# One chunk of the ffn ring and four of the mixer ring moved onto the split weights' 128 byte lines, and products of ones placed at six waits of TensorE

## The chip, the cores and the metric

The kernel runs on one core of a Trainium2 chip, in one launch. The metric is device microseconds of that launch, the median of several runs; lower is better. The notes below call the engines as the profile does: PE is TensorE (matmuls), PEld its weight loads, DVE VectorE, ACT ScalarE, SP the engine that issues most of the DMAs.

## What is computed

A sequence of 256 tokens with 1024 channels goes through two models one after the other, in fp32. Cut to what matters here:

```python
# first_block: a gmlp layer, then an attention layer, each followed by a mixture of experts
x = x + g1 * gmlp_mixer(modulate(rmsnorm(x), sh1, sc1), ...)       # layer 0
x = x + g2 * moe(modulate(rmsnorm(x), sh2, sc2), ...)              # 64 experts, 8 per token
x = x + g1 * moba_mixer(...)                                       # layer 1: attention over 256 keys
x = x + g2 * moe(...)
x = rmsnorm(x) * final_norm
# second_block, twice:
x = x + 0.5 * swiglu_ffn(rmsnorm(x), w_up, w_down)                 # 1024 -> 2 x 2816 -> 1024
x = x + hybrid_mixer(rmsnorm(x), ...)                              # pooling + gated linear recurrence
x = x + 0.5 * swiglu_ffn(rmsnorm(x), w_up, w_down)
# and a last rmsnorm
```

## The kernel before

**Order of the work.** The program is one list of items, emitted in order: gmlp, the experts of layer 0 (moe), attention, the experts of layer 1, then for each of two layers an ffn, the hybrid mixer and a second ffn. Each item names the weights that it reads, its PE work and what follows on ACT and DVE. PE executes its instructions in the order of this list and waits at each for its operands, so whatever is emitted ahead of a waiting matmul runs ahead of it. Channels lie on the 128 partitions, the 256 tokens on the free axis.

**Weights.** They stream from HBM through SP's queue into a ring of nine slots of 1 MB (line 177). For the dense layers each slot is split into a rounded high part `WH` (an ACT copy, line 243) and a low part `WL` (a DVE subtraction, line 246), two halves of 1024 columns each. A product is then three matmuls of 128 x 128 weights by 128 x 256 moving data: `WH` by the activations' high part, `WH` by their low part, `WL` by their high part (`mm3`, line 290; all go through `mm`, line 288).

**Where operands lie.** `ring`, `WH`, `WL` and `x` are whole multiples of 128 bytes per partition. After them comes a pad of 64 bytes (`pad0`), then `hH` and `hL`, the split input of a stage (8 chunks of 256 tokens each, 1 KB per chunk), then a second pad of 64 bytes. `hH` and `hL` therefore lie half of a 128 byte line off from `WH` and `WL`. The arena `rarena`, allocated last, also lies half a line off (the offsets that the change adds rest on that). Its views begin at multiples of 1 KB or of 128 bytes, so all of them are half a line off too. Among them are the ring of an ffn's hidden chunks, `hid_ring(0, 6)` (line 543): six chunks of high parts, then six of low parts; the mixer's rings `vH, vL` (ten chunks, also used for `yH, yL`) and `pH, pL` (four chunks, also used for `mH, mL`); and `SHU1`, in which the moe keeps half of the shared expert's up weights, as weights this time (line 729).

**An ffn** (`swiglu_items`, line 785) has 22 up items of 48 matmuls, which read `hH, hL`, and 11 down items of 48 matmuls (`down_d`, line 396), which read chunks 2i and 2i+1 (mod 6) of the ring: for every down but the last, first the 24 matmuls of the even chunk, then the 24 of the odd one. Chunk 0 is so read by downs 0, 3, 6 and 9. Downs and ups alternate, one down to two ups.

**The mixer** (`hybrid`, line 1584): projections from `hH, hL`; `smallA`, which reads v chunks 0 to 5 (six matmuls each); `smallB`, which reads v chunks 6 to 9 and the four p chunks; the pool-up items, which read p; then `lru_up`, where each of eight output chunks is a sum over the ten y chunks in order (30 matmuls), and the out projection, which reads the m chunks.

**Moe.** For each block of tokens the gather (line 1097) multiplies by `WH`-side weights with moving data in `rarena`. The shared expert's `shared_mm` (line 1039) uses, for j = 2 and 3, weights from `SHU1` with `hH, hL` as moving data: the one place where weights and moving data are both half a line off.

**Waits of PE around the change.** In gmlp, PE waits between the first vector-matrix products and the first projection, while DVE and ACT make `hH, hL` (`mod_h`, line 367). In each routing stage it waits for DVE to choose the experts (line 938) ahead of `route1b` (line 940). At the end of layer 1's moe (`scat_last`, line 1184) it waits for the first chunk of the first ffn's input. At the start of attention it waits three times: ahead of the sums of squares (`stat_mm`), ahead of the row of inverse roots (`stat_row`), and ahead of the first chunk that `norm` makes (line 1319).

Of the kernel before, what the change touches and what calls it, by code (L numbers as in the profile page):

```python
# [18 lines left out]
T = 256  # L19
# [1 line left out]
KD = 8  # L21
NRING = 9
FW = 6656
RW = 7168
HCAP, MCAP, LCAP = 10, 9, 9
RMS_EPS = 1e-6
LN_EPS = 1e-5
# [67 lines left out]
def moba_moe_hybrid_kernel(ctx: ExitStack, tc: tile.TileContext, A: dict):  # L95
# [50 lines left out]
    def rview(off, n):  # L146

        assert off + n <= RW, (off, n)
        return rarena[:, off:off + n]
# [42 lines left out]
    def add(pe, post=(), slots=(), lead=0, fence=(), nsplit=2):  # L192
        post = [] if post is None else [post] if callable(post) else list(post)
        items.append(Item(list(slots), pe, post, st["nring"], fence, lead, nsplit))
# [95 lines left out]
    def mm3(out, w, h, l, start, stop, swap=False):  # L290
        wh, wl = w
        for j, (a, b) in enumerate(((wh, h), (wh, l), (wl, h))):
            if swap:
                a, b = b, a
            mm(out, a, b, start and j == 0, stop and j == 2)

    def to_hl(src, H, L):
        S.copy(H, src)  # L298
        V.tensor_sub(L, src, H)  # L299
# [36 lines left out]
    def stat_mm(sqs, b=STB):  # L336

        for m in range(KD):
            c = 32 * (m % 4)
            mm(PB[b][c:c + 32, :T], ones[:, :32], sqs[m], m < 4, m >= 4, tile_position=(0, c))  # L340
# [12 lines left out]
    def stat_row(p=None):  # L353
        p = PB[STB][:, :T] if p is None else p
        for t in range(2):
            P.transpose(p[:, t * 128:(t + 1) * 128], nv[:, 1, t:t + 1].to_broadcast([128, 128]), ident)
        S.copy(R, p)
# [9 lines left out]
    def mod_h(Ac, Bc, H, L, ks=range(KD)):  # L367

        ts = {}

        def low(k):
            V.scalar_tensor_tensor(L[:, k], ts.pop(k), Bc[:, k:k + 1], H[:, k], op0=ALU.add, op1=ALU.subtract)
        for i, k in enumerate(ks):
            t = ts[k] = tmp512()[:, :T]
            V.scalar_tensor_tensor(t, x[:, k], Ac[:, k:k + 1], R, op0=ALU.mult, op1=ALU.mult)
            S.activation(H[:, k], t, AF.Identity, bias=Bc[:, k:k + 1])
            if i:
                low(ks[i - 1])
        low(ks[-1])
# [147 lines left out]
    def add_all(lst):  # L527
        for it in lst:
            add(*it)
# [13 lines left out]
    def hid_ring(off, n):  # L543
        Hs = rview(off, n * T).rearrange("p (n t) -> p n t", n=n)
        Ls = rview(off + n * T, n * T).rearrange("p (n t) -> p n t", n=n)
        return Hs, Ls

    def gmlp():
        v = spare(5, 4096).rearrange("p (t f) -> p t f", t=2)
        u = spare(5, 4096, 4096).rearrange("p (m t) -> p m t", m=16)  # L550
# [30 lines left out]
        for i, it in enumerate(first):  # L581
            add(*(it + (None, ()))[:3], nsplit=0)
            if i == 1:
                add(stats, nsplit=0)
                add(lru_consts, nsplit=0)
        add(load, nsplit=0)

        add(lambda: scale_cols(0, sc1(0), "nmix", 0), nsplit=1)
        add(lambda: mod_h(Acol[:, 0], sh1(0), hH, hL))
# [259 lines left out]
    def moe(l, tail):  # L849
# [162 lines left out]
        side = gemv_items(3, adac[:, 1, 0:16], "adab", 48, 5) if l == 0 else gemv_half(1, g2(1), "adab", 88, 5)  # L1012
        g0, g1_ = ((4, 4), (0, 0))[l]
        add_all(side[:g0])
        add(route1b)
        add_all(side[g0:g1_])
        add(route2)
# [166 lines left out]
        def scat_last(tail):  # L1184
            def pe():
                b = NB - 1
                for k in range(KD):
                    fs = slice(k * 128, (k + 1) * 128)
                    for j, y in enumerate((yH, yL)):
                        mm(PB[4 + k // 2][:, k % 2 * T:(k % 2 + 1) * T], y[:, fs], STm[:, b % 3], j == 0, j == 1)  # L1190
                tail(lambda k: upd(k, PB[4 + k // 2][:, k % 2 * T:(k % 2 + 1) * T]))
            add(pe, fence={yb // 2}, nsplit=l)

        def scat(b):
# [51 lines left out]
        def upd(k, y):  # L1246
            V.scalar_tensor_tensor(x[:, k], y, g2(l)[:, k:k + 1], x[:, k], op0=ALU.mult, op1=ALU.add)
# [53 lines left out]
    def attention():  # L1301
# [16 lines left out]

        def norm():
            stat_row()  # L1320
            mod_h(Acol[:, 1], kvc[:, 0:8], kvH, kvL)

        side = gemv_items(4, adac[:, 1, 16:32], "adab", 64, 0) + gemv_half(0, sc2(1), "adab", 80)
# [3 lines left out]
        def gemvs(m, nsplit=2):  # L1327
            nonlocal n
            for it in side[n:n + m]:
                add(*(it + (None, ()))[:3], nsplit=nsplit)  # L1330
            n += m

        gemvs(3, 0)
        add(lambda: stat_mm(sqs_of["x"]), nsplit=0)
        add(stat_sum, nsplit=0)
        add(norm)
        ring_slots(0, 1, 2, 3, 4)

# [214 lines left out]
            V.scalar_tensor_tensor(x[:, k], x[:, k], cols[:, o + k:o + k + 1], R1, op0=ALU.mult, op1=ALU.mult)  # L1553

    def first_ffn(fin):
        hidH, hidL = hid_ring(0, 6)
        sums = lambda: (stat_mm(sqs_of["x"]), stat_mm(sqs_of["y"], 1))
        lst = swiglu_items("f1u", 0, "f1d", 0, 22, hidH, hidL, evac_R, fin, 6,
                           [{"korder": True, "before": lambda: sqs_of["first"]()}, {"after": sums}, {"mid": first_sums}, {"mid": first_rows, "bank": 3}], lag=4)
        for i, n in enumerate((8, 10, 12, 14)):  # L1560
            pe, post, slots, lead = lst[n]
            lst[n] = (pe, list(post or []) + [lambda i=i: first_x(2 * i, 2 * i + 1)], slots, lead)
        add_all(lst)
# [13 lines left out]
            nc.sync.dma_start(A["out"][k], y)  # L1577

    def ffn(l, which, fin):
        hidH, hidL = hid_ring(0, 6)  # L1580
        nm = f"f{which}"
        add_all(swiglu_items(nm + "u", 22 * l, nm + "d", 11 * l, 22, hidH, hidL, evac_R, fin, 6))

    def hybrid(l, fin):
# [5 lines left out]
        gates = spare(6, 4096).rearrange("p (n f) -> p n f", n=8)  # L1590
        up_ = spare(6, 2 * 288, 5376).rearrange("p (b t) -> p b t", b=2)
        pw = spare(6, 4 * 288, 4096).rearrange("p (b t) -> p b t", b=4)
        vH, vL = hid_ring(0, 10)
        yH, yL = vH, vL
        pH, pL = hid_ring(5120, 4)
        mH, mL = pH, pL
        sp4 = lruc[:, 5, l * 10:(l + 1) * 10]
        nsp8 = lruc[:, 0, l * 10:(l + 1) * 10]
# [310 lines left out]
```

## Time and profile before

| | |
|---|---|
| three timed runs | 2549.05, 2557.68, 2557.32 us; median 2557.32 |
| the profiled execution's own time | 2549.97 us |
| its span, first to last instruction | 2548.0 us |
| PE busy | 2421.7 us (95%) |
| DVE, ACT busy | 1359.7 us (53%), 1041.7 us (41%) |
| HBM read | 720.50 MB |
| mean granted TensorE clock | 0.988 of full speed |

Times in the profile are microseconds from the start of the span. A view of windows gives, for each stretch, the busy time of each engine with the number of instructions, then the clock that was granted to TensorE (1.00 is 2.4 GHz, 0.50 is 1.2 GHz), the share of the DMA engines that was busy, and GB/s. Matmuls are pipelined: one takes about 0.28 us from start to end, but the next starts after about 0.115 us. So the cost of a dense stretch is read from starts: the length of the stretch by its matmuls. A window counts matmuls that reach in from the left as well, two or three. In the timeline a row is: start, busy time, engine, line, operation, operands (moving data, then weights), count, and in brackets the idle time of the engine just before and what ended it.

### The profile page before, as it was taken

What the parts mean: (1) busy time and instruction counts of PE and PEld (TensorE: products, weight loads), DVE (VectorE), ACT (ScalarE), POOL (GpSimd) and SP (SyncE); (2) the same over time, 40 slices, a digit from 0 to 9 for tenths busy, and PEclk for the clock granted to TensorE, in tenths of its full rate; (3) what the DMA queues carried; (4) which work ended last, traced back from release to release, by engine and by line L of the source; (5) the groups of instructions that cost most, each with busy time, mean ns of one, the idle gap of its engine ahead of it and who ended that gap; (6) DMA issues with size and microseconds to landing.
All of it is one profiled execution on the core that took longest, in us unless ns stands there. A gap on an engine that the chain in (4) does not pass through costs nothing. (4 is left out here: it accounts for less than half of the span.)

```text
span 2548.0 us, 43865 instructions
## 1 busy us (share of the span) xinstructions
PE 2421.7 (95%) x17938; PEld 1885.0 (74%) x17938; DVE 1359.7 (53%) x2536; ACT 1041.7 (41%) x1710; POOL 3.8 (0%) x6
## 2 busy tenths in 40 slices
PE   6998999999989979999999899999999999999998
PEld 4885545544448845454544899999999999999998
DVE  4556223333257642333332765788756656887665
ACT  3334222222235532222221544585544545685543
POOL 0000000000000000000000000000000000000000
PEclk8999999999999989999999999999999999999999
DMA  9877999999967389999999554453755554444750
GB/s 393 316 280 320 389 420 420 420 414 421 421 278 269 145 346 406 420 420 418 418 421 420 197 183 149 162 192 136 281 191 191 191 191 149 174 171 171 267 187 17
DMA packets 101437, 724.45 MB, mean 284 GB/s; under 512 B 11248, under 2 KB 12528, under 8 KB 14192
## 3 DMA queue, kind: packets, MB, share of 16 engines
q1 hardware_dynamic: 100080, 718.32, 71.2%
q8 instruction: 143, 2.34, 0.4%
q10 hardware_dynamic: 1152, 3.28, 0.3%
q14 instruction: 62, 0.51, 0.1%
HBM read 720.50 MB, written 1.05 MB: 283 GB/s over the span
## 5 line engine op out<-in xcount | busy, mean ns | idle before, releaser
L288 PE MATMUL pb<-rarena,WH 128*128 128x256 f32 x3552 | 698.3, 283 | 26.3 <-DVE farena L1207 21.9
L243 ACT CAST WH<-ring 128x1024 fp32r<-128x1024 f32 x476 | 489.4, 1047 | 427.2 <-PE pb L288 340.9
L288 PE MATMUL pb<-hH,WH 128*128 128x256 f32 x2336 | 653.1, 280 | 9.6 <-DVE farena L1008 6.3
L288 PE MATMUL pb<-hH,WL 128*128 128x256 f32 x2336 | 649.9, 278 | 3.1 <-DVE WL L246 3.1
L246 DVE TENSOR_TENSOR WL<-ring,WH 128x1024 fp32r<-128x1024 f32 x476 | 570.7, 1215 | 148.5 <-ACT WH L243 145.7
L288 PE MATMUL pb<-hL,WH 128*128 128x256 f32 x2336 | 649.7, 278 | 0.1
L288 PEld LDWEIGHTS pb<-rarena,WH 128*128 128x128 f32 x3552 | 574.3, 189 | 43.7 <-ACT farena L1110 27.1
L288 PE MATMUL pb<-rarena,WL 128*128 128x256 f32 x2224 | 589.2, 280 | 4.5 <-DVE WL L246 3.1
L288 PEld LDWEIGHTS pb<-hH,WH 128*128 128x128 f32 x2336 | 439.1, 188 | 22.3 <-issue 10.2
L288 PE MATMUL pb<-ring,farena 128*32 128x512 f32 (+2 forms) x2064 | 431.7, 595 | 15.4 <-DMA ring<-ex 15.4
L288 PEld LDWEIGHTS pb<-hH,WL 128*128 128x128 f32 x2336 | 439.0, 188 | 4.7 <-DVE WL L246 4.5
L288 PEld LDWEIGHTS pb<-hL,WH 128*128 128x128 f32 x2336 | 438.9, 188 | 0.4 <-DVE hL L1509 0.3
L288 PEld LDWEIGHTS pb<-rarena,WL 128*128 128x128 f32 x2224 | 419.6, 189 | 6.4 <-DVE WL L246 3.7
L288 PEld LDWEIGHTS pb<-ring,farena 128*32 128x32 f32 (+2 forms) x2064 | 136.5, 130 | 228.3 <-issue 186.7
L1147 DVE SCALAR_TENSOR_TENSOR tmp<-pb,small,tmp 128x256 f32<-128x256 f32 x56 | 27.1, 484 | 396.2 <-ACT tmp L1145 396.2
L288 PE MATMUL pb<-ring,tmp 128*32 128x512 f32 (+2 forms) x1024 | 223.2, 598 | 8.8 <-DMA ring<-ex 4.8
L288 PEld LDWEIGHTS pb<-ring,tmp 128*32 128x32 f32 (+2 forms) x1024 | 68.6, 129 | 158.4 <-issue 135.2
L1180 DVE TENSOR_TENSOR WL<-pb,WH 128x512 fp32r<-128x512 f32 x112 | 77.5, 692 | 172.3 <-ACT WH L1179 172.3
L1207 DVE TENSOR_TENSOR farena<-farena,pb 128x512 f32<-128x512 f32 x208 | 133.6, 684 | 65.3 <-PE pb L288 65.3
L831 DVE TENSOR_TENSOR tmp<-pb,R 128x512 f32<-128x512 f32 x88 | 60.8, 691 | 184.8 <-PE pb L288 181.0
L1179 ACT CAST WH<-pb 128x512 fp32r<-128x512 f32 x112 | 65.7, 586 | 178.2 <-PE pb L288 174.7
L1161 ACT COPY tmp<-pb 128x256 f32<-128x256 f32 x56 | 20.8, 372 | 287.8 <-PE pb L1159 287.8
(301 smaller groups left out, 1705.4 us busy)
## 6 DMA issues: line engine op xcount, KB each, us to landing
ring<-ex SPq DMA_DIRECT2D x384, 1024.0 KB, 12.6
ring<-ada SPq DMA_DIRECT2D x56, 1024.0 KB, 8.3
ring<-f1u SPq DMA_DIRECT2D x44, 1024.0 KB, 4.8
ring<-f2u SPq DMA_DIRECT2D x44, 1024.0 KB, 4.9
ring<-win SPq DMA_DIRECT2D x40, 1024.0 KB, 4.8
ring<-f1d SPq DMA_DIRECT2D x22, 1024.0 KB, 4.8
ring<-f2d SPq DMA_DIRECT2D x22, 1024.0 KB, 4.9
ring<-lu SPq DMA_DIRECT2D x10, 1024.0 KB, 4.8
```

The lines of the kernel that those rows point to most:

```text
L243: S.copy(hi, raw)
L246: V.tensor_sub(lo, raw, hi)
L288: P.matmul(out, l, r, start=start, stop=stop, skip_group_check=True, **kw)
L831: V.tensor_tensor(t.rearrange("p (a t) -> p a t", a=2), hold["p"].rearrange("p (a t) -> p a t", a=2), R.rearrange("p (o t) -> p o t", o=1) ...
L1147: V.scalar_tensor_tensor(hh, bank[:, 256:], wsl[:, b % 2:b % 2 + 1], t[:, :256], op0=ALU.mult, op1=ALU.mult)
L1161: S.copy(t, bank[:, :256])
L1179: S.copy(yH[:, fs], PB[DN[f]])
L1180: V.tensor_tensor(yL[:, fs], PB[DN[f]], yH[:, fs], op=ALU.subtract)
L1207: V.tensor_tensor(a2, a2, bank, op=ALU.add)
```

## The change

The class `Chunks` gives a ring in which chunks below `on` begin 64 bytes after the old offset, that is on the 128 byte line, and the others 128 bytes after it, half a line off as before. The ffns' ring is made with `on` = 1: chunk 0 of the high parts and chunk 0 of the low parts lie on the line. The mixer's v and y ring is made with `on` = 4; its p ring moves by 64 elements and stays half a line off, and the arena grows by 64 elements. gmlp, attention and moe keep their places. `keep_warm(n, b)` issues n matmuls of a 128 x 128 matrix of ones (bf16) by 512 columns of ones into PSUM bank b, where nothing reads them. Seven calls at six places: 16 in gmlp, 6 and 20 ahead of `route1b` (layers 0 and 1), 10 at the end of layer 1's moe, and 7, 10 and 5 at the three waits of attention.

```diff
-RW = 7168
+RW = 7232
...
+    def keep_warm(n, b):
+        r = onesb.rearrange("p (o n) -> p o n", o=1).to_broadcast([128, 4, 128])
+        for _ in range(n):
+            mm(PB[b], onesb, r, True, True)
...
+    class Chunks:
+        def __init__(self, off, n, on):
+            self.off, self.n, self.on = off, n, on
+        def __getitem__(self, key):
+            c = key[1]
+            a, m = (c.start, c.stop - c.start) if isinstance(c, slice) else (c, 1)
+            assert a >= self.on or a + m <= self.on
+            v = rview(self.off + (16 if a < self.on else 32) + a * T, m * T)
+            return v.rearrange("p (n t) -> p n t", n=m) if isinstance(c, slice) else v
+    def lined_ring(off, n, on):
+        return Chunks(off, n, on), Chunks(off + n * T + 32, n, on)
...
         add(load, nsplit=0)
+        add(lambda: keep_warm(16, 0), nsplit=0)
...
         add_all(side[:g0])
+        add(lambda: keep_warm((6, 20)[l], 4))
         add(route1b)
...
                 tail(lambda k: upd(k, PB[4 + k // 2][:, k % 2 * T:(k % 2 + 1) * T]))
+                if l == 1:
+                    keep_warm(10, 2)
...
         def norm():
             stat_row()
+            keep_warm(5, 2)
             mod_h(Acol[:, 1], kvc[:, 0:8], kvH, kvL)
...
         gemvs(3, 0)
+        add(lambda: keep_warm(7, 2), nsplit=0)
         add(lambda: stat_mm(sqs_of["x"]), nsplit=0)
         add(stat_sum, nsplit=0)
+        add(lambda: keep_warm(10, 2), nsplit=0)
         add(norm)
...
     def first_ffn(fin):
-        hidH, hidL = hid_ring(0, 6)
+        hidH, hidL = lined_ring(0, 6, 1)
...
     def ffn(l, which, fin):
-        hidH, hidL = hid_ring(0, 6)
+        hidH, hidL = lined_ring(0, 6, 1)
...
-        vH, vL = hid_ring(0, 10)
+        vH, vL = lined_ring(0, 10, 4)
         yH, yL = vH, vL
-        pH, pL = hid_ring(5120, 4)
+        pH, pL = hid_ring(5184, 4)
```

## Rows read from the trace of the kernel before

**Rows 1.** The page, parts 1 and 2 (40 slices of 63.7 us).

```profile
PE 2421.7 (95%) x17938; PEld 1885.0 (74%) x17938; DVE 1359.7 (53%) x2536; ACT 1041.7 (41%) x1710; POOL 3.8 (0%) x6
...
PEclk8999999999999989999999999999999999999999
DMA  9877999999967389999999554453755554444750
```

**Rows 2.** Windows: stretches of the ffns and mixers; columns as told above, all engines.

```profile
1454.00:1616.00 162.00, 162.00 (x1377) 161.94 (x1375) 99.75 (x136) 78.89 (x111) 0.00 (x0) 1.00 0.46 169
...
1635.40:1677.40 42.00, 42.00 (x372) 42.00 (x372) 40.22 (x82) 26.70 (x44) 0.00 (x0) 1.00 0.54 195
1677.60:1704.00 26.40, 26.40 (x226) 26.40 (x226) 18.82 (x30) 24.70 (x36) 0.00 (x0) 1.00 0.54 200
1751.00:1798.80 47.80, 47.80 (x408) 47.80 (x407) 33.80 (x53) 20.91 (x30) 0.00 (x0) 1.00 0.39 144
1822.90:1980.70 157.80, 157.80 (x1394) 157.80 (x1394) 97.73 (x126) 77.36 (x104) 0.00 (x0) 1.00 0.56 198
...
2188.40:2258.70 70.30, 70.30 (x598) 70.30 (x598) 60.41 (x112) 53.07 (x80) 0.00 (x0) 1.00 0.53 192
...
2376.60:2534.00 157.40, 157.40 (x1391) 157.40 (x1390) 94.77 (x122) 74.65 (x100) 0.00 (x0) 1.00 0.38 135
```

**Rows 3.** Timeline of PE: weights from the arena, then a gather, layer 0.

```profile
420.42 0.40 PE L288 MATMUL pb<-hH,rarena 128*128 128x256 f32 x2
...
422.34 0.28 PE L288 MATMUL pb<-rarena,WH 128*128 128x256 f32 x1
...
424.95 0.28 PE L288 MATMUL pb<-rarena,WL 128*128 128x256 f32 x1
```

**Rows 4.** Timeline of PE: a gather with no such work ahead of it.

```profile
1302.06 0.28 PE L288 MATMUL pb<-rarena,WL 128*128 128x256 f32 x1
...
1304.65 0.28 PE L288 MATMUL pb<-rarena,WL 128*128 128x256 f32 x1
```

**Rows 5.** Windows: three of the stretches at the lower clock.

```profile
30.70:40.80 10.10, 5.49 (x25) 4.85 (x24) 8.30 (x19) 5.44 (x9) 0.00 (x0) 0.50 1.01 418
...
750.90:760.90 10.00, 6.29 (x27) 5.66 (x28) 8.11 (x27) 4.57 (x10) 0.00 (x0) 0.50 0.62 256
...
1450.60:1453.80 3.20, 3.06 (x14) 3.06 (x15) 2.73 (x6) 1.43 (x3) 0.00 (x0) 0.50 0.13 20
```

**Rows 6.** Timeline at the start of gmlp: PE, and DVE's last chunk of hL.

```profile
30.41 1.01 PE L477 MATMUL pb<-cst,rows 128*128 128x128 f32 x4 [0.71 <-ACT rows L473]
36.03 0.58 PE L288 MATMUL pb<-WH,hH 128*128 128x256 f32 x1 [4.61 <-ACT hH L376]
...
41.43 0.49 DVE L372 SCALAR_TENSOR_TENSOR hL<-tmp,adac,hH 128x256 fp32r<-128x256 f32 x1 [0.18 <-ACT hH L376]
...
44.18 1.06 PE L288 MATMUL pb<-ring,silc 128*32 128x512 f32 x8
```

**Rows 7.** Timeline at the start of attention: PE, and DVE's last chunk of kvL.

```profile
748.37 1.07 PE L288 MATMUL pb<-tmp,ones 128*32 128x256 f32 x16 [1.96 <-DVE Acol L1472]
...
753.09 0.69 PE L356 MATMUL pb<-cst,nv 128*128 128x128 f32 x2 [2.49 <-DVE nv L325]
755.30 1.10 PE L288 MATMUL pb<-rarena,WH 128*128 128x256 f32 x2 [1.52 <-ACT rarena L376]
...
760.69 0.48 DVE L372 SCALAR_TENSOR_TENSOR rarena<-tmp,kvc,rarena 128x256 fp32r<-128x256 f32 x1 [0.18 <-ACT rarena L376]
...
763.87 1.06 PE L288 MATMUL pb<-ring,silc 128*32 128x512 f32 x8
```

**Rows 8.** Timeline of PE: the waits of the two routing stages and of the first ffn.

```profile
227.08 0.22 PE L288 MATMUL pb<-farena,onesb 128*128 128x64 bf16 x2 [1.33 <-DVE farena L938]
...
896.15 0.27 PE L288 MATMUL pb<-farena,onesb 128*128 128x64 bf16 x2 [4.89 <-DVE farena L938]
...
1414.26 0.39 PE L288 MATMUL pb<-hH,WH 128*128 128x256 f32 x1 [2.38 <-ACT hH L1512]
```

## The prediction, made before the changed kernel was run

> **What bounds the kernel now.** I read the page first. PE is busy 95% of the span, at full clock but for a few slices, and the DMA engines are full only in the two expert stages (slices 5 to 11 and 16 to 23) [rows 1]. Outside these, PE's stream is the path, and a saving there counts in full. Ahead of the experts it counts too, since their transfers start only when the experts are chosen. Inside them it doesn't.
>
> Next I read dense stretches by windows, dividing length by matmuls. The ffn at 1822.9 has 1392 matmuls (1394 less two that reach in) in 157.8 us: **113.4 ns** from start to start. The last ffn has the same, 157.4 us for 1389. The first ffn has 1375 in 162.0 us: **117.8 ns**. Same instructions, same clock 1.00, no stall in any of them [rows 2]. So a matmul of 256 columns has two steady paces, 4.4 ns apart, and a stretch keeps the one in which it started. The mixers show where it can change. Layer 0's projections run at 113.5 ns (42.0 us for 370), wait briefly for a late `WL` half, and go on at about 117.7 (26.4 us for 224); the stretches at 1751 and 2188.4 are at the slow pace all through (47.8 us for 406, 70.3 for 596) [rows 2].
>
> In all these the weights lie on the line and the moving data half a line off. One place has both half a line off: the shared expert in the moe. There 16 matmuls take 1.92 us, **120.0 ns** each, and the gather that follows without a gap, back at the usual placement, runs 23 matmuls in 2.61 us, **113.5 ns** [rows 3]. A gather without such a piece ahead of it runs 22 matmuls in 2.59 us, 117.7 ns [rows 4]. Of this piece the trace has four, two in each layer, and behind each the next matmuls run at the quick pace. This is what the change's first part does in the ffns: a short piece with both operands placed alike, then the usual placement.
>
> Last I read the clock. At the start of gmlp and of attention it stands at 0.50 for about 10 us, and falls for 3 us more in the first ffn [rows 5].
>
> **The change, part by part.** The sum is made against the profiled execution, 2549.97 us, which is 7.35 below the median 2557.32 and 0.92 above the fastest run. Two of three runs lie near 2557.5. An ffn at the slow pace costs 1390 x 4.4 ns = 6.1 us more than one at the quick one, so one ffn that landed differently would make most of that difference; this I can't see in one profile.
>
> *First ffn.* From the first down on, at 1454, the 162.0 us become 72 matmuls at 120 (chunk 0 in downs 3, 6 and 9) and 1303 at 113.4: 8.6 + 147.8 = 156.4. **-5.6 us.** Down 0 runs partly at the lower clock [rows 5]; if the pace turns only at down 3, some 50 us later, -4. The pace of matmuls with both operands on the line is in no row; the nearest is both half off, 120 [rows 3], and the other bound is 113.4, no cost. I take 120, since the two operands stand to each other in the same way.
>
> *Three other ffns.* They are quick already (two of them in rows 2; the one at 2004.6 has the same pace). Each gets 96 matmuls at 120 instead of 113.4: +0.63, together **+1.9**; bound 0.
>
> *Mixers.* In `lru_up` four of ten y chunks lie on the line. The stretch at 1751 holds seven whole output chunks (84 matmuls on the line) and the out projection: 84 x 120 + 322 x 113.4 = 46.6 instead of 47.8, -1.2, in both layers -2.4. The next ffn's 47 matmuls up to its first stall become quick, -0.2 twice. `smallA` costs 24 x 6.6 ns = +0.16 in layer 0, where it is quick now. In layer 1 it turns the stretch at 2188.4; as in layer 0 I let the quick pace last 194 matmuls, up to a late `WL`: -0.8. Together **-3.6**. Bounds: 0, if twelve matmuls are too few to turn the pace, to -4.5, if layer 1's stretch stays quick.
>
> *Products of ones.* No row has such a matmul; two matmuls of 256 columns take 2 x 117.8 = 0.24 us, at half clock 0.47. I use that as price. They run while PE waits, so they cost nothing where the wait is longer: in attention 7 x 0.24 = 1.7 in a wait of 1.96, 10 in 2.49, 5 x 0.24 = 1.2 in 1.52 [rows 7]; in routing 6 x 0.24 = 1.4 in 1.33 and 20 x 0.24 = 4.7 in 4.89; ahead of the first ffn 2.4 in 2.38 [rows 8]. The banks that they write are free there. If they ran at half clock they would overrun each wait by as much again, and the matmul behind them, with all that waits for it, would be late by 1 to 4 us. Both routing waits and the last stand behind work at full clock, so I take no delay.
>
> What they give: in attention the projection starts at 755.30 and the next work at 763.87; its 48 matmuls run mostly at half clock. At full clock they follow `norm`, whose last low part is ready at 760.69 + 0.48 = 761.2; then half a us of matmuls, end 761.7: **-2.2** [rows 7]. In gmlp likewise: the last low part is ready at 41.92, end 42.5 instead of 44.18. But there the clock is already down when the sixteen start at about 31.2. Before, it was up again 4.8 us after the first matmul (36.03 to 40.8); so count eleven at 0.43 to 0.47 and five at 0.24, ready at 37.3 at worst, 48 matmuls at 118 then end by 43.0 at worst: **-1.5**, bounds +0.2 (all sixteen slow) and -1.7 [rows 5, 6]. In the routing stages and ahead of the first ffn: **0**, since behind them transfers decide, or ACT and DVE do. Together -3.7.
>
> **Sum**: -5.6 + 1.9 - 3.6 - 3.7 = -11.0; 2549.97 - 11.0 = **2539**. What is late next: DVE's `WL` halves in the mixers.
>
> **The rivals.**
>
> *The slow pace follows (slower).* The piece on the line could hand over to the slow pace rather than the quick one; both operands on the line has no row, only both off. Place: chunk 0 of every ffn. Price: the three quick ffns go to 96 at 120 and about 1295 at 117.8, +6.4 each, 19.2; the first ffn +0.2, the mixers +1.5. 2549.97 + 20.9 - 3.7 = 2567. It decides as soon as one ffn turns, since 6.4 is more than the products of ones give. For it: the slow pace is where most stretches land after a stall. Against it: all four pieces in the trace hand over to the quick one [rows 3]. 10%.
>
> *Placement does nothing.* The two paces could come from how a stretch starts, and rows 3 against rows 4 from the missing stall. Then the first part changes nothing: 2549.97 - 3.7 = 2546. Against it: 120.0 is a pace that no other stretch shows, and only the placement differs there. 14%. The Trainium skill, "TensorE: Matmul & The Clock Gate", section "Step-by-step: what each phase is for", speaks for this rival: TensorE reads the moving operand and the weights through two independent ports, so how the two lie to each other should not matter. By that rule alone the first part would be worth nothing; rows 3 speak against it.
>
> *The slower runs stay.* If what makes two of three runs 7.35 us longer is no ffn at the slow pace but something that the change doesn't touch, the median is 2539 + 7.35 = 2546. For it: one profile can't show it. Against it: a whole ffn's pace is 6.1. 12%.
>
> *The products of ones don't hold the clock*, or stand in the way by as much as they give: 2539 + 3.7 = 2543, inside my range.
>
> **How the numbers follow.** A measurement of this kernel can tell about 0.5% from no change: faster means below 2544.5, slower above 2570. My forecast has 62%, with its own range 2533 to 2544: down by the mixers' bound, by the fall of the clock in the first ffn if it goes, and by what a quick pace in other stretches would give, up by the two bounds on the first ffn and gmlp. The second and third rivals (26%) and most of the first (10%) lie between 2546 and 2570, so within 0.5%. Faster 0.62, same 0.33, slower 0.05. For 8 in 10 the range takes in both rivals at 2546 with their own spread: 2533 to 2554.
>
> **What would show it.** In the changed profile the first ffn from its first down on runs in about 156.4 us, quick but for pieces of 24 matmuls at about 120; the other ffns become 0.6 longer each; `lru_up` shows 12 at 120 and 18 at 113.4 in turn; the clock is 1.00 from 751 to 761 and the first projection of attention ends 2 us sooner. I am wrong if matmuls of chunk 0 keep the pace of their neighbours, if stretches after them run at 117.8, or if matmuls behind the products of ones start later than their operands are ready.

## The result, and the profile after

The changed kernel takes **2569.88 us** (median of 4 runs, 2566.80 to 2571.08), the kernel before, with one more run, 2554.56 (4 runs, 2549.05 to 2557.68). The ratio is 1.0064, with an interval from 1.0051 to 1.0078: slower by 0.6%, and above the predicted range. The profiled execution after took 2566.80 us with a span of 2564.8, 16.8 longer than the profiled one before.

The page's first part and its clock row of the changed kernel; they answer to [rows 1]:

```profile
PE 2455.9 (96%) x18012; PEld 1909.0 (74%) x18012; DVE 1359.8 (53%) x2536; ACT 1042.0 (41%) x1710; POOL 3.8 (0%) x6
...
PEclk9998999999999999999999999999999999999999
```

PE has the 74 products of ones more and is busy 34 us longer; DVE, ACT and POOL do what they did. The clock row shows a 9 at both places that had an 8 before. Its one new 8, in the fourth slice, comes from two falls to 0.50, one for 3.4 us at 195 us and one for 10 us at 230 us, of which the profiled run before had the second alone; a second profile of the kernel before (`e17_before_again`) has the same 8 there. From the first ffn on, the clock falls at the same two places before and after: for 3.4 us in the first ffn, and at the end of the span, where PE has no work. So the loss is PE's own, at full clock. To see where it lies, I cut both spans at the first matmul of each stage. The timeline of PE in the kernel before, at the starts of the mixer, the second ffn, the third ffn (layer 1), the mixer and the last ffn (the first ffn's start is in [rows 8]):

```profile
1610.33 0.28 PE L288 MATMUL pb<-hH,WH 128*128 128x256 f32 x1
...
1798.80 0.28 PE L288 MATMUL pb<-hH,WH 128*128 128x256 f32 x1
...
1980.72 0.28 PE L288 MATMUL pb<-hH,WH 128*128 128x256 f32 x1
...
2163.50 0.36 PE L288 MATMUL pb<-hH,WH 128*128 128x256 f32 x1 [0.91 <-ACT tmp L334]
...
2352.44 0.28 PE L288 MATMUL pb<-hH,WH 128*128 128x256 f32 x1
```

The same starts in the changed kernel, with the first ffn's ahead of them:

```profile
1411.99 0.38 PE L288 MATMUL pb<-hH,WH 128*128 128x256 f32 x1 [0.21 <-ACT hH L1541]
...
1607.98 0.28 PE L288 MATMUL pb<-hH,WH 128*128 128x256 f32 x1
...
1797.09 0.28 PE L288 MATMUL pb<-hH,WH 128*128 128x256 f32 x1
...
1985.24 0.28 PE L288 MATMUL pb<-hH,WH 128*128 128x256 f32 x1
...
2174.24 0.36 PE L288 MATMUL pb<-hH,WH 128*128 128x256 f32 x1 [0.69 <-ACT tmp L340]
...
2363.25 0.28 PE L288 MATMUL pb<-hH,WH 128*128 128x256 f32 x1
```

The differences of these rows, stage by stage:

| stage | before | after | change | predicted |
|---|---|---|---|---|
| up to the first ffn | 1414.26 | 1411.99 | -2.3 | -3.7 |
| first ffn | 196.07 | 195.99 | -0.1 | -5.6 |
| mixers, layers 0 and 1 | 188.47, 188.94 | 189.11, 189.01 | +0.6, +0.1 | -3.6 together |
| second, third, last ffn | 181.92, 182.78, 195.6 | 188.15, 189.00, 201.6 | +6.2, +6.2, +6.0 | +1.9 together |

So the three ffns that were quick lose 18.4 us, and nothing else moves much. (The mixers' +0.7 is no more than two executions differ by: in the second profile of the kernel before they take 189.1 and 189.2.) Windows of the changed kernel show the first ffn, the 72 up matmuls ahead of the second ffn's first down, the rest of that ffn, and the last one; they answer to [rows 2]:

```profile
1451.70:1613.70 162.00, 162.00 (x1377) 161.89 (x1375) 99.83 (x136) 78.96 (x111) 0.00 (x0) 1.00 0.46 169
1813.10:1821.20 8.10, 8.10 (x74) 8.10 (x73) 5.00 (x9) 5.52 (x9) 0.00 (x0) 1.00 0.86 357
1821.20:1985.20 164.00, 164.00 (x1394) 164.00 (x1394) 97.93 (x127) 77.46 (x104) 0.00 (x0) 1.00 0.53 191
...
2375.00:2538.00 163.00, 163.00 (x1389) 163.00 (x1388) 97.05 (x128) 77.11 (x102) 0.00 (x0) 1.00 0.43 159
```

The first ffn shows the same 162.00 us for 1375 matmuls as before: 117.8 ns. The second one starts quick (8.10 us for about 72) and then takes 164.00 for 1392, **117.8 ns** where it had 113.4. The timeline has the turn, at the first down:

```profile
1821.14 0.28 PE L288 MATMUL pb<-hH,WL 128*128 128x256 f32 x1
1821.26 0.40 PE L288 MATMUL pb<-rarena,WH 128*128 128x256 f32 x2
...
1824.11 0.39 PE L288 MATMUL pb<-rarena,WH 128*128 128x256 f32 x2
...
1826.93 0.28 PE L288 MATMUL pb<-hH,WH 128*128 128x256 f32 x1
```

The 24 matmuls of chunk 0 take 2.85 us (118.8 each), the 24 of chunk 1, which is half a line off as before, 2.82 (117.5), and the up matmuls behind them stay at 117.8 to the end of the ffn. Chunk 0 itself costs little; the slow pace that follows it costs 6 us per ffn.

### The profile page after: what moved, and what is told of

Read it like the earlier page. It is cut to its first block, busy times and chain, and to the rows that moved or that the text cites. A ratio compares the mean times of both kernels' runs of the same rounds, so it can differ in the third digit from the quotient of the medians.

```text
span 2564.8 us, 44013 instructions
## 1 busy us (share of the span) xinstructions
PE 2455.9 (96%) x18012; PEld 1909.0 (74%) x18012; DVE 1359.8 (53%) x2536; ACT 1042.0 (41%) x1710; POOL 3.8 (0%) x6
```

## Addresses

The compiled program gives the offsets per partition (the sizes of the tiles, in the order in which the kernel allocates them, give the same distances): `WH` 90240, `WL` 106624, `hH` 131264, `hL` 139456, `rarena` 197824 bytes. Modulo 256, `WH` and `WL` lie at 128 and the other three at 192. So before, all moving data of the ffns lay **64** bytes on from the weights modulo 256, high and low parts alike. After, chunk 0 lies 128 on (high) and 0 on (low), and the other chunks 192 on (high) and 64 on (low): the ring's low parts start 32 elements further on, so they move by 192 bytes (chunk 0) and 256 bytes (the others), not by 64 and 128 like the high parts, and the two no longer lie alike. "Half a line off as before" holds modulo 128 bytes, not modulo 256. A theory must therefore say which it is: chunk 0 on the 128 byte line (A), or any other distance modulo 256, or unlike parts (B).

## The experiments

The time up to the first ffn differs by up to 10 us between profiles: in the twenty profiles of this study the first ffn starts at 1410.4 to 1420.1, in two of the kernel before at 1414.3 and 1416.0. (The first routing is reached at 225.0 to 230.1, and each of the two expert stages differs by 3 to 4 us.) So beside the ratio to the kernel before I give the **dense part**, from the first ffn's first matmul to the end of the span, in one profile each: 1133.7 before and 1152.8 after.

**Each part alone, and two other placements.** `e1_fill` keeps the products of ones and puts the rings back; `e2_rings` keeps the rings and takes the products of ones out. `e3_same256` and `e4_shift` change only the offsets (in elements) in the class, high below `on`, high above, low below, low above; in `e4_shift` no chunk is on the line (`on` = 0):

```diff
-            v = rview(self.off + (16 if a < self.on else 32) + a * T, m * T)
+            v = rview(self.off + (self.low if a < self.on else self.high) + a * T, m * T)
...
+        return Chunks(off, n, on, 48, 64), Chunks(off + n * T, n, on, 112, 128)   # e3_same256
+        return Chunks(off, n, on, 0, 32), Chunks(off + n * T, n, on, 32, 64)      # e4_shift, on = 0
```

> The products of ones alone, every ring where it was before. Both theories say the same of this run: the three ffns that were quick (113.4 ns a matmul) stay quick, the first ffn stays at 117.8, the input of the first ffn is ready 2.3 us sooner as in the changed kernel, so about 2548 us in the profile (2549.97 - 2.3). If the products of ones are what turns the ffns slow, it comes out near 2566.

> The moved rings alone, no products of ones. Theory A (a chunk on the 128 byte line hands over to the slow pace) and theory B (what counts is where moving data and weights lie to each other modulo 256 bytes, and in the changed ring high and low parts no longer lie alike) both expect all four ffns at 117.8 ns and 2566.8 + 2.3 = 2569 us. If the pace was set by the products of ones, it stays at 2550.

> The change with other offsets: chunk 0 of the ffn ring and chunks 0 to 3 of the mixer ring lie, in high and low parts, at the same place modulo 256 bytes as the split weights, as weights and moving data of the shared expert do; all other chunks 64 bytes on from the weights modulo 256, as before. Both are on the 128 byte line or half a line off just as in the change. Theory A: all ffns slow, 2567 us. Theory B: matmuls of chunk 0 at about 120 ns, the rest quick in all four ffns, first ffn from its first down on 156 us instead of 162: 2540 us.

> The change with no chunk on the line: all high parts of the ffn and mixer rings moved by 128 bytes, all low parts by 256, as the change moves the chunks that it leaves half a line off. Theory A: nothing on the line, ffns as before, about 2548 us. Theory B: high and low parts lie differently modulo 256 bytes, so no down keeps the quick pace, all four ffns at about 117.8 ns: 2567 us.

Measured: `e1_fill` 2550.71 us, ratio 0.9994 (0.9981 to 1.0006), dense part 1130.6; `e2_rings` 2574.30, 1.0085 (1.0067 to 1.0103), 1152.7. The whole loss is the rings'. `e3_same256` 2573.62, 1.0077 (1.0057 to 1.0096), 1154.4; `e4_shift` 2570.24, 1.0069 (1.0051 to 1.0087), 1152.5. A window of the second ffn of `e3_same256`, behind its first down:

```profile
1826.00:1984.00 158.00, 158.00 (x1343) 158.00 (x1343) 92.82 (x118) 75.00 (x99) 0.00 (x0) 1.00 0.54 192
```

And of `e4_shift`:

```profile
1820.00:1980.00 160.00, 160.00 (x1361) 160.00 (x1361) 94.28 (x118) 75.05 (x98) 0.00 (x0) 1.00 0.54 189
```

Both are at 117.8 ns (158.00 by 1341, 160.00 by 1359). With no chunk on the line the pace is lost as well, so A alone falls; with chunk 0 alike in both parts and no distance modulo 256 it is lost too, so B as I had it falls. What is left is theory C: any place but 64 bytes on ends the quick pace.

`e3_same256` is also the piece that the prediction had in mind, built into an ffn: chunk 0 lies like the weights in both parts, and the usual placement follows. The windows of its chunk 0 and of the chunk behind it, in the second ffn's first down, ahead of which the ffn is quick:

```profile
1830.02:1832.90 2.88, 2.88 (x27) 2.88 (x26) 2.88 (x5) 2.62 (x4) 0.00 (x0) 1.00 0.17 23
1832.90:1835.73 2.83, 2.83 (x27) 2.83 (x26) 2.83 (x5) 1.36 (x2) 0.00 (x0) 1.00 0.85 347
```

The bounds are starts, so three of each 27 reach in: 24 matmuls at 120.0 ns, the pace of the shared expert's piece [rows 3], and then 24 at 117.9. The piece hands over to the slow pace.

**A control, and both parts alike at two other distances.** Only the offsets differ:

```diff
+        return Chunks(off, n, on, 0, 64), Chunks(off + n * T, n, on, 0, 64)     # e6_all256, on = 0
+        return Chunks(off, n, on, 0, 32), Chunks(off + n * T, n, on, 0, 32)     # e7_all128, on = 0
+        return Chunks(off, n, on, 16, 64), Chunks(off + n * T, n, on, 80, 128)  # e5_line128
```

> A control: all chunks of the ffns' and the mixers' v and y rings moved by 256 bytes, high and low parts alike, so that modulo 256 nothing lies otherwise than before; products of ones kept. Theory C: three ffns quick and one slow as with the products of ones alone, 2546 to 2555. Rival D (places modulo 256 do not matter; what ends the quick pace is something that the moved rings share, the longer arena or the views made chunk by chunk): four slow ffns, about 2570.

> All chunks of these rings moved by 128 bytes, high and low parts alike: half a line off as before, but 192 instead of 64 bytes on from the weights modulo 256. Theory C: the first down of each ffn ends the quick pace, about 2570. Theory A (only a place on the 128 byte line ends it): three quick ffns, about 2550. Theory B2 (unlike high and low parts end it): three quick ffns, about 2550.

> As the change, but chunk 0's low part lies where its high part lies, both 128 bytes on from the weights modulo 256, and all other chunks lie 64 bytes on modulo 256 as before. Theory C (the quick pace lasts only while both parts lie 64 bytes on from the weights modulo 256, as they did before; 24 matmuls of a down that lie otherwise end it, and nothing in an ffn brings it back): all four ffns at 117.8 ns from their first down on, median about 2572. Theory A (chunk 0 on the line ends it): the same. Theory B2 (what ends it is that high and low parts do not lie alike; 128 on, for both, hands over to the quick pace): four quick ffns, about 2542.

Measured: `e6_all256` 2549.94 us, 0.9992 (0.9980 to 1.0004), dense part 1134.3; `e7_all128` 2559.81, 1.0038 (1.0023 to 1.0053), 1145.8; `e5_line128` 2568.49, 1.0071 (1.0054 to 1.0088), 1153.4. The second ffn of `e6_all256` from its first down on:

```profile
1824.10:1981.90 157.80, 157.80 (x1395) 157.80 (x1394) 97.71 (x126) 77.32 (x104) 0.00 (x0) 1.00 0.56 197
```

That is the row of before, 113.3 ns. The same class, the same longer arena and another absolute place, but the same place modulo 256: the pace is kept. So it is the place modulo 256 that matters, and rival D falls. In `e5_line128` the same stretch is slow:

```profile
1822.00:1986.00 164.00, 164.00 (x1394) 164.00 (x1393) 97.89 (x127) 77.40 (x104) 0.00 (x0) 1.00 0.54 191
```

`e7_all128` lies between, as no theory expected. Its windows show two up items, the down behind them, two more up items, and the last two downs of the first ffn:

```profile
1826.80:1838.10 11.30, 11.30 (x98) 11.30 (x97) 5.53 (x7) 4.93 (x6) 0.00 (x0) 1.00 0.60 206
1838.10:1843.60 5.50, 5.50 (x51) 5.50 (x50) 4.85 (x6) 2.83 (x4) 0.00 (x0) 1.00 0.49 179
1843.60:1854.90 11.30, 11.30 (x99) 11.30 (x98) 4.86 (x6) 4.93 (x6) 0.00 (x0) 1.00 0.53 188
1596.60:1607.90 11.30, 11.30 (x98) 11.30 (x97) 9.03 (x16) 6.52 (x12) 0.00 (x0) 1.00 0.54 187
```

With both parts 192 bytes on, the first down does turn the up items to 117.7, but from the second down on the downs run at 113.5 (the 48 matmuls of the second row take 5.45 us from start to start, 1838.13 to 1843.58) between slow up items, whose operands no run moved, and in the first ffn the same downs run at 117.7. So theory C holds in that the first down of another placement ended the quick pace wherever it was tried, and falls in that 117.8 then holds for all that follows. The runs don't separate what the moving data's place is measured against: the weights and `hH, hL` never moved, so it could be the distance to the weights, the distance to `hH, hL`, or the place itself. For the distance to the weights speaks only that 120.0 ns came out at two different places where moving data and weights lie alike: 192 for both in the shared expert, 128 for both in chunk 0 of `e3_same256`.

**Does the piece with both operands half a line off turn the pace by itself?** The prediction rested on this. `e8_turn` is `e1_fill` with such a piece in the first ffn:

```diff
+                if i == 0 and dname == "f1d" and d0 == 0:
+                    for n in range(24):
+                        mm(acc_ap(0), hidH[:, 0, (n % 2) * 128:(n % 2 + 1) * 128], hH[:, n % KD], True, True)
```

> The rings of before with the products of ones, and in the first ffn, ahead of its first down, 24 extra matmuls with weights from the ring's chunk 0 and moving data from hH, both half a line off as in the shared expert's piece; their sums are overwritten by the down's first matmul. If such a piece by itself hands over to the quick pace: it costs 24 x 0.12 = 2.9 us, and the first ffn's 1300 matmuls behind it run at 113.4 instead of 117.8, 5.7 us less, so 2.8 us faster than with the products of ones alone, the first ffn 159.2 us. If the turn in the moe had another cause (the short stop or the weight buffer that follows there): the first ffn stays at 117.8 and takes 164.9 us, 2.9 us slower.

Measured: 2549.88 us, 0.9986 (0.9976 to 0.9996), dense part 1131.5. Its windows of the piece, and of the first ffn behind it:

```profile
1450.30:1453.20 2.90, 2.90 (x26) 2.90 (x25) 1.49 (x3) 1.38 (x3) 0.00 (x0) 1.00 0.00 0
1453.20:1611.50 158.30, 158.30 (x1346) 158.30 (x1345) 98.16 (x132) 75.07 (x101) 0.00 (x0) 1.00 0.48 171
```

24 matmuls at 120.0 ns, as in [rows 3] (by their starts, 1450.33 to 1453.21), and then 158.30 us for 1344: 117.8. The piece by itself does not hand over the quick pace. (It cost no time either: it lies in a wait of 2.34 us for `WL` that `e1_fill` has there.) In the moe the same piece is followed by 113.3 ns at all four places in all twenty profiles, so something else must come with it there; what it is isn't shown.

**Can a break turn it back?** Behind the two transposes of `stat_row`, in the middle of the third up item of three ffns and of both mixers, the next 72 matmuls run at 113.3 ns in all twenty profiles. `e9_two` and `e10_four` put two and four such transposes ahead of the first ffn's sixth up item, `e13_mid` two in its middle, into `stat_row`'s bank; `e11_mix` and `e14_midmix` add two ahead of the mixers' item behind `smallA` (`e11_mix` also ahead of `lru_up`); `e12_same2` and `e15_same_mid` put them behind the chunk 0 downs of `e3_same256`. All but the last two have the rings of before, and all have the products of ones. The edit, here of `e9_two`, and of `e13_mid`:

```diff
+            for t in range(turn):
+                P.transpose(hold["p"][:, t % 2 * 128:(t % 2 + 1) * 128], nv[:, 1, t % 2:t % 2 + 1].to_broadcast([128, 128]), ident)
             proj_b(w, hold["p"], hH, hL, korder, mid)
...
+            if turn:
+                mid2 = lambda: [P.transpose(PB[STB][:, t * 128:(t + 1) * 128], nv[:, 1, t:t + 1].to_broadcast([128, 128]), ident)
+                               for t in range(2)]
+            proj_b(w, hold["p"], hH, hL, korder, mid2 if turn else mid)
```

> The rings of before with the products of ones, and in the first ffn, ahead of its sixth up item (right behind the first down), two transposes as stat_row issues them; their sums are overwritten at once. In every trace so far the 72 matmuls of 256 columns behind stat_row's two transposes ran at 113.3 ns, whatever ran before them. Theory E (two such transposes set the quick pace, and with operands 64 bytes on from the weights modulo 256 it stays): the first ffn goes from 117.8 to 113.4 for some 1300 matmuls, 5.7 us less, for 0.3 us of transposes; median about 2545. Rival F (the quick pace comes from something else at those places, or the first ffn is kept slow by something of its own): 117.8 stays, about 2551.

> The same with four transposes, as many as first_rows issues in the first ffn, behind which 72 matmuls ran at 117.8 in every trace so far. If it is their number that sets the pace: the first ffn stays at 117.8, about 2551. If any short break with transposes turns it: as with two, about 2545.

> As with two transposes in the first ffn, and two more ahead of the mixers' first item behind smallA and ahead of lru_up, in both layers. Theory E: behind them 420 and some 480 matmuls of each mixer run at 113.4 until the next stall, where the products of ones alone show 117.8 in most of them: 1.8 and 2.1 us less each, for 0.3 us each, where they were slow; 2538 to 2543. Rival F: about 1 us slower than the products of ones alone, 2552.

> The rings in which chunk 0 lies on the line with no distance from the weights modulo 256 (2573.62 before, four slow ffns), and two transposes ahead of the first up item behind each down that reads chunk 0 but the last. Theory C with E (24 matmuls at another place end the quick pace, nothing but a break brings it back): chunk 0 at 119 to 120 in downs 0, 3, 6 and 9, everything else at 113.4 up to the next such down; about 2561. Rival (chunk 0's place slows what follows in another way, so that transposes do not help): about 2576.

> The rings of before with the products of ones, and in the first ffn two transposes in the middle of the sixth up item, after its eighth triple and into the bank that stat_row uses: the break behind which every trace so far shows 113.3 ns. Theory G (this break sets the quick pace wherever it stands): the first ffn runs at 113.4 from there, 5.6 us less for 0.3 us; median about 2545. Rival F (the first ffn is kept slow by something of its own): 2551 as before.

> As e13_mid, and two transposes ahead of the mixers' first item behind smallA, behind which 372 matmuls ran at 113.3 in both layers of the run e11_mix. Theory G: another 1.6 us less for 0.3 in each mixer that lands at 117.8 there; 2541 to 2544. Rival F: 2548 to 2550.

> Chunk 0 on the line with no distance from the weights modulo 256, all else as before, and the break of e13_mid in the first up item behind downs 0, 3 and 6 of every ffn. If the slow pace is only a state that the break undoes: downs 0, 3, 6 and 9 at 118 to 119, 113.4 from each break to the next such down; about 2560. If it is kept up by the placement: 2574 to 2577.

| run | median us | ratio (interval) | dense part |
|---|---|---|---|
| `e9_two` | 2549.77 | 0.9988 (0.9972 to 1.0003) | 1133.3 |
| `e10_four` | 2549.53 | 0.9989 (0.9975 to 1.0002) | 1133.5 |
| `e11_mix` | 2549.77 | 0.9982 (0.9966 to 0.9999) | 1134.7 |
| `e12_same2` | 2571.64 | 1.0076 (1.0054 to 1.0098) | 1155.1 |
| `e13_mid` | 2548.36 | 0.9985 (0.9976 to 0.9994) | 1132.0 |
| `e14_midmix` | 2550.51 | 0.9991 (0.9982 to 1.0000) | 1132.9 |
| `e15_same_mid` | 2573.95 | 1.0081 (1.0066 to 1.0097) | 1156.7 |

In the first ffn of these runs no break turned the slow pace. The window of `e13_mid` behind its break:

```profile
1460.60:1610.50 149.90, 149.90 (x1275) 149.90 (x1274) 89.58 (x120) 69.57 (x93) 0.00 (x0) 1.00 0.47 168
```

149.90 us for 1273: 117.8. Of the twelve breaks in the ffns of `e12_same2`, and as many of `e15_same_mid`, none turned it either. In the mixers of `e11_mix` both did, layer 0 and layer 1:

```profile
1654.30:1696.50 42.20, 42.20 (x375) 42.20 (x373) 33.88 (x63) 33.26 (x52) 0.00 (x0) 1.00 0.56 194
2208.10:2250.30 42.20, 42.20 (x375) 42.20 (x374) 33.89 (x63) 33.21 (x52) 0.00 (x0) 1.00 0.56 194
```

In those of `e14_midmix`, with the same break at the same place, neither did:

```profile
1658.80:1702.70 43.90, 43.90 (x375) 43.90 (x374) 35.68 (x65) 34.97 (x54) 0.00 (x0) 1.00 0.53 187
2212.40:2256.30 43.90, 43.90 (x375) 43.90 (x374) 35.68 (x65) 34.93 (x54) 0.00 (x0) 1.00 0.53 186
```

373 matmuls take 42.20 us (113.1) in the one and 43.90 (117.7) in the other. Ahead of `lru_up` the break of `e11_mix` turned the pace in layer 1, for the 24 matmuls up to the next wait, and not in layer 0. Theories E and G fall as rules: the same transposes give the quick pace at some places and not at others. But they are not without effect. In the seventeen profiles that have no break behind `smallA`, the pace behind it was never quicker than ahead of it; with the break it was, in both layers of `e11_mix`.

**The program or the execution?** Three kernels once more, unchanged, one profile each.

> The kernel of e11_mix once more. If the program sets the pace at each place: the same, 372 matmuls at 113.3 ns behind smallA in both layers. If the execution does: 117.8 behind it in one or both.

> The kernel before once more. If the program sets the pace at each place: three quick ffns, the first at 117.8, the mixers as in the first profile (216 and 194 quick in layer 0, 72 in layer 1). If the execution does in the mixers: the ffns the same, the mixers' quick stretches of other lengths, and the time off by up to 6 us for it.

> The changed kernel once more. If chunk 0 and the unlike chunks end the quick pace by where they lie: all four ffns at 117.8 from the first down again, 2566 to 2571. If the four slow ffns were the luck of one execution: one or more of them quick.

`e16_mix_again` took 2543.42 us, the kernel before beside it 2548.98; the same two windows of its mixers:

```profile
1651.00:1693.90 42.90, 42.72 (x377) 42.52 (x376) 34.59 (x64) 33.94 (x53) 0.00 (x0) 1.00 0.54 191
2204.60:2248.80 44.20, 44.20 (x378) 44.20 (x377) 35.99 (x66) 35.25 (x54) 0.00 (x0) 1.00 0.53 185
```

Quick in layer 0, now slow in layer 1 (ahead of `lru_up` its breaks did as in `e11_mix`): in the mixers the execution decides. It does so at the start of the first ffn too. The windows of that ffn's first down, and of what follows the two transposes behind it:

```profile
1447.00:1452.00 5.00, 5.00 (x46) 5.00 (x46) 4.49 (x8) 3.16 (x6) 0.00 (x0) 1.00 0.46 164
1452.40:1604.40 152.00, 152.00 (x1293) 152.00 (x1292) 92.37 (x122) 71.03 (x94) 0.00 (x0) 1.00 0.47 170
```

Here the first down is quick (44 matmuls in 5.00 us; from start to start 113.3), where `e1_fill`, `e9_two` and `e14_midmix`, at clock 1.00 all through, have 117.8; and behind the break it is 117.7. So a break can end the quick pace as well, and nothing of the first ffn's own keeps its first down slow, as rival F had it.

In the other three ffns the execution does not decide. `e17_before_again` (2552.56 us, dense part 1134.5) has the second ffn of before, and the mixers at 117.8 behind their first 72 matmuls in both layers:

```profile
1825.50:1983.30 157.80, 157.80 (x1394) 157.80 (x1394) 97.73 (x126) 77.57 (x104) 0.00 (x0) 1.00 0.56 198
```

and `e18_after_again` (2568.27 us, dense part 1152.9) has that of the changed kernel:

```profile
1822.10:1986.10 164.00, 164.00 (x1395) 164.00 (x1394) 97.93 (x126) 77.30 (x104) 0.00 (x0) 1.00 0.53 190
```

## Why the prediction was wrong

**The step that failed** is "a short piece with both operands placed alike, then the usual placement", taken to hand over to the quick pace. The four places in the moe do so every time, but in the ffns it did not: in `e3_same256`, where chunk 0 is such a piece, 120.0 ns are followed by 117.9 in an ffn that was quick up to there, and in `e8_turn` a piece of the same length and the same 120.0 ns left a slow ffn slow. So the piece is not what sets the pace. I took four cases at two places of one loop for a rule, although each of them differs from an ffn in more than the placement.

- *First ffn, -5.6*: it stayed at 117.8, -0.1. No placement and no break that was tried gave it the quick pace beyond its first down, so this change had nothing to win there.
- *Three other ffns, +1.9*: +18.4. That is the first rival, "the slow pace follows": its place (chunk 0, from the first down), its price (6.4 each, measured 6.0 to 6.2) and its time (2567 against the profiled 2566.80) came out. That the time fits so closely is partly luck, since its other terms were off both ways (mixers +1.5 against +0.7, products of ones -3.7 against -2.3 up to the first ffn). I gave it 10%. What I held against it was the piece in the moe alone. That my mechanism was an inference from a different loop, while "both on the line" had no row at all, should have made the two about equally likely. I also overlooked that the change moves *every* chunk of the ring by a distance that differs between high and low parts; `e4_shift` shows that this alone costs as much as the whole change.
- *Pace of chunk 0, 120 ns*: 118.8 in the first down. I took 120 because the two operands stand to each other as in the shared expert; modulo 256 only the low part does. Where both parts do (`e3_same256`) it is 120.0. The term is small.
- *Mixers, -3.6* (the terms given add up to -3.5): +0.7. A step that leaned on the same rule. The two profiles of the kernel before show besides that the execution moves the mixers: 194 quick matmuls behind `smallA` in one and none in the other.
- *Products of ones, -3.7*: right in attention, right in gmlp in some executions only; the next paragraph has the rows.
- *Placement does nothing* (14%) falls by `e6_all256` against `e4_shift`. By the Trainium skill, "TensorE: Matmul & The Clock Gate", section "Step-by-step: what each phase is for", weights and moving data come through two independent read ports. What I worked out from it for this rival, that their placement should not matter, the runs do not bear out: with the rings 128 bytes on (`e7_all128`) the dense part takes 1145.8 us, with 256 bytes (`e6_all256`) 1134.3, and the measurement decides.
- *The slower runs stay* (12%): the two profiles of the kernel before, 2549.97 and 2552.56 us, differ by 1.8 us up to the first ffn and by 0.8 behind it, and both have three quick ffns. What made two of the first three runs 7 us longer was not profiled; the later batches of the kernel before, 17 to 25 runs each, have medians of 2552.2 to 2553.8.

In this profile the products of ones did what the working said. In windows of the two stretches at the start of gmlp and of attention the clock no longer falls [rows 5]; the fourth row is a fall that comes later in gmlp:

```profile
30.70:40.80 10.10, 8.45 (x53) 5.98 (x51) 8.43 (x19) 5.50 (x10) 0.00 (x0) 1.00 1.02 420
748.70:758.70 10.00, 8.31 (x57) 5.23 (x58) 6.18 (x25) 3.74 (x9) 0.00 (x0) 1.00 0.90 372
1448.00:1451.40 3.40, 2.94 (x14) 2.95 (x15) 2.93 (x6) 1.32 (x3) 0.00 (x0) 0.50 0.08 19
...
195.30:198.80 3.50, 3.50 (x19) 3.50 (x18) 3.46 (x7) 0.00 (x0) 0.00 (x0) 0.51 0.61 180
```

The third row is the first ffn's, which has none at that place and keeps its fall. The timeline of the changed kernel answers to [rows 6 to 8]:

```profile
30.76 0.59 PE L288 MATMUL pb<-onesb 128*128 128x512 bf16 x2
...
42.63 0.64 PE L288 MATMUL pb<-ring,silc 128*32 128x512 f32 x4
...
226.73 0.22 PE L288 MATMUL pb<-farena,onesb 128*128 128x64 bf16 x2
...
748.96 1.07 PE L288 MATMUL pb<-tmp,ones 128*32 128x256 f32 x16 [0.35 <-DVE Acol L1501]
...
755.62 0.91 PE L288 MATMUL pb<-rarena,WH 128*128 128x256 f32 x2 [0.44 <-ACT rarena L382]
...
762.39 0.64 PE L288 MATMUL pb<-ring,silc 128*32 128x512 f32 x4
...
893.91 0.22 PE L288 MATMUL pb<-farena,onesb 128*128 128x64 bf16 x2 [0.57 <-DVE farena L961]
```

gmlp's projection ends at 42.63 instead of 44.18 (-1.55; predicted -1.5). Of this 0.35 is left at the first routing (226.73 instead of 227.08): the fall at 195.30, which the profiled run of before lacks and its second one has, costs an estimated 1.7 us, half of its 3.5. Attention takes 13.43 us from its sums of squares to the end of its projection (748.96 to 762.39), where it took 15.50 (748.37 to 763.87): -2.07, predicted -2.2. The second routing comes at 893.91 instead of 896.15, and the first ffn starts 2.3 us sooner. Attention's gain is in all seventeen profiles with the products of ones, 13.4 us against 15.4 to 15.5 in the three without. Gmlp's is not: in seven of the seventeen the clock still falls there for 3.4 us, and in six of these, a second profile of the changed kernel (`e18_after_again`) among them, the projection ends about 1 us later than here. In the total all this drowns in the up to 10 us by which the time up to the first ffn differs between executions: `e1_fill` alone gives 0.9994, not clear of no change. But eight kernels have the products of ones and keep the quick pace in three ffns (`e1_fill`, `e6_all256` and `e8_turn` to `e14_midmix` without `e12_same2`), most with a small addition, and their ratios run from 0.9982 to 0.9994 with a mean of 0.9988: 3 us, the size of the predicted 3.7.

The best versions are the products of ones with the rings of before: `e11_mix`, `e13_mid` and `e8_turn` beat both kernels, the one before by 0.14 to 0.18% with intervals that end below 1, but by no more than the products of ones explain.

**What stays open**: what gives a stretch its pace when it starts. Shown is that behind `stat_row`'s break it is quick at all five places in all twenty profiles, that in the mixers behind `smallA`, and in the first ffn's first down, the execution decides, that a first down at another place modulo 256 ends the quick pace, and that a piece or a break like those ahead of quick stretches doesn't bring it back reliably: in the mixers it did at some places, in the ffns at none, and once it ended it. Whether the place counts by its distance to the weights is not shown. A cause within TensorE is in no row here.

## What to carry to other kernels

Moving an operand "by half a line" or a whole one is not neutral. Before reading a change of placement, list the address of every operand modulo 256 bytes, for each part of a split product, and measure a control that moves the same buffers by a distance that should not matter. A pattern that holds at four places of one loop is one case, not four: reproduce it by itself at the place where it is to be used, since a piece of 24 matmuls shows within one profile whether it does there what it seemed to do elsewhere. And where the part ahead varies by 10 us from execution to execution, compare the part behind it.

## What the runs showed of the hardware that was not expected

- Which of the two paces of a 256 column fp32 matmul, 113.3 or 117.8 ns, an ffn keeps depends on where its moving data lie modulo 256 bytes (given here as distance to the weights, which never moved): the dense part is 1130.6 to 1134.7 us in all eleven profiles with 64 bytes (the mixers' paces differ among these), and 1152.5 to 1156.7 in the eight in which the distances of high and low parts differ or chunk 0 lies on the line.
- With 192 bytes for both parts, pace goes by item: downs at 113.5 and up items at 117.7 in turn, for a whole ffn, 1145.8 us.
- With 256 bytes more, nothing changes: 1134.3.
- With moving data and weights alike modulo 256, pieces of 24 matmuls run at 119.4 to 120.1 ns: in the shared expert, in `e8_turn`, and in chunk 0 of `e3_same256`, `e12_same2` and `e15_same_mid`.
- A break of two transposes can change the pace either way: 117.8 to 113.3 in both mixers of `e11_mix`, 113.3 to 117.8 in the first ffn of the same kernel run again.
